# Attention with split scores: two heads at a time on the two halves of the array's rows, and the normalisation moved to VectorE

## The chip, the cores and the metric

The kernel runs on one core of one Trainium2 chip. The metric is device time in microseconds of one execution; where a kernel was run several times the median is given. A core has five engines with a queue of their own each: TensorE (PE, with its weight loads shown apart as PEld), VectorE (DVE), ScalarE (ACT), GpSimd (POOL) and SyncE (SP, which here only starts the loads of weights). Every engine takes its instructions in the order in which they were written into its queue, and waits on semaphores for the others.

## The reference: what is computed

A trunk of two layers on 256 tokens of 1024 features, in float32. Each layer is a SwiGLU half-step, a mixer, and another SwiGLU half-step, every one behind an RMSNorm and added to the residual stream. Both mixers have 16 heads of 64. Cut to what matters here:

```python
def swiglu(h, w_gate, w_up, w_down):              # 1024 -> 2816 -> 1024
    return (silu(h @ w_gate) * (h @ w_up)) @ w_down

# mixer A: three dilated causal windows, merged per head by their softmax denominators
s = einsum('...qd,...kd->...qk', q, k) * HEAD_DIM ** -0.5;  p = softmax(where(mask, s, -inf))
o = einsum('...qk,...kd->...qd', p, v);  out = o @ w_o

# mixer B: q from its own projection, k and v computed once from the stream after layer 0;
# with 256 tokens there is one block, so that it is plain causal attention
```

In the kernel both are one softmax per head over the keys: the three windows of mixer A become one additive mask (the logarithm of how many windows hold the pair), and mixer B has the causal mask.

## The kernel before, in words

Names and lines are those of the profile. 256 tokens are two tiles of 128 (`t`), the 1024 features eight blocks of 128. The precision comes from splitting: `parts_of` (L90) writes a float32 value as the sum of two float32r parts, the high one by a copy on ACT (L92), the low one by a subtraction on DVE (L94, or L96 with a scale). Weights are split in the same way by `pieces_of` (L154 on ACT, L155 on DVE, 1024 columns at a time, eight pieces in flight), and a product of two split operands is three float32r products: high by high, high by low, low by high (L183, L185, L187 for tokens on partitions; L192, L193, L195 for features on partitions).

Only the scores are not split. `attend` takes a list of groups of four heads and, per head:

- `scores` (L490): q^T and k^T are plain float32, two heads to a tile of 128 partitions, so that one head has 64 rows. Two products: queries of tile 0 with 128 keys, queries of tile 1 with 256 keys, both into one PSUM bank. The program's float32 product is two passes of the array, so that the trace has four matmuls for a head.
- softmax: a masked, scaled negative with the row maximum on DVE (L492, two instructions with an accumulator read each), the exponential with the row sum on ACT (L495, two), the reciprocal on DVE (L497), and the normalisation on **ACT** (L499, one instruction of 128 columns and one of 256).
- three transposes of p (L510) into a PSUM bank, split into `pT` by `parts_of`.
- the product with v (L527 to L530): v is split into high and low parts, which are two stationary operands. Each is loaded with **both heads of a pair** side by side (128 columns), of which only the own half of the result is used. Four matmuls of 512, 256, 256 and 256 columns. The two halves of the result's bank are added by a copy on ACT (L536) and an addition on DVE (L537).
- each pair's o^T is split (`oT`) and is an input of the output projection `out_t` (L418 to L420), which holds four of the five PSUM banks of the pool `accp`.

PSUM has eight banks: five in `accp`, three in `trp`. A score bank, a bank of transposes of p and a bank of transposes of q and k all come from `trp`.

What sets the order: `weave` merges two generators of steps. The main one is `attend`, the filling one is the projection of the next group's q, k and v (mixer A, groups 0 to 2), or the output projection (mixer A, group 3), or the second half of the queries' projection followed by the output projection (mixer B, all four groups as one stream). Each step yields the time of TensorE that its author put to it, and the merge spreads the one stream over the other; so TensorE always has other products between a head's scores, its transposes and its product with v. `AHEAD` is how many heads have their scores ahead of their transposes, `LATE` how many heads the product with v comes late. The framework then fixes one order of instructions for each engine when the program is built. In mixer A a group is opened by the projection of q and k: `turned` scales and rotates them (L459, L451 to L454), `transposed` (L468) turns them and copies them on DVE to `qT` and `kT` (L470). Mixer B reads k^T from `kTb`, written by the shared projection, and splits v for each group when it comes to it (`bv`, L92 and L94).

Of the kernel before, what the change touches and what calls it, by code (L numbers as in the profile page):

```python
# [15 lines left out]
P = 128  # L16
S = 256
# [11 lines left out]
AHEAD = 3  # heads whose scores are there ahead of their transposes  # L29
LATE = 1  # heads by which the products with v follow the transposes  # L30
EXTRA = 1  # blocks of an output projection that wait for the end of the attention
# [10 lines left out]
def shape_constants():  # L42
    """Rotary tables and attention masks: functions of the shapes alone."""
# [23 lines left out]
def trunk(ctx: ExitStack, tc: tile.TileContext, a: dict, out: bass.AP):  # L67
# [6 lines left out]
    ap_ = ctx.enter_context(tc.tile_pool(name="ap", bufs=22))  # L74
# [15 lines left out]
    def parts_of(hi, lo, src, scale=1.0):  # L90
        """src * scale as the sum of two float32r parts."""
# [48 lines left out]
    def unit(name, k, n, srcs):  # L140
        """Loads [P, k, n] of weights and splits it into pieces of 1024 columns."""
# [18 lines left out]
    def opening(wg, wu, before):  # L160
        """The first two units, in parts of two blocks of rows that arrive with the parts of x."""
# [18 lines left out]
    def product(accs, xh, xl, ws, first, last):  # L180
        """accs[i] += x @ ws[i] for one block of 128 rows of the contraction."""
# [7 lines left out]
    def product_t(ac, wh, wl, x, first, last):  # L189
        """ac[:, 0] + ac[:, 1] += w^T @ x^T for one block of 128 rows of the contraction; x: [P, hi and lo, S]."""  # L190
# [69 lines left out]
    def some(steps, n):  # L260
        """The next n steps."""
# [5 lines left out]
    def hurried(steps, factor):  # L267
        """Steps that a weave takes sooner than their time says."""
# [3 lines left out]
    def weave(main, main_total, fill, fill_total):  # L272
        """Traces both streams, the steps of the one spread over those of the other."""
# [14 lines left out]
    def down_t(name, w, blocks, norm):  # L288
        """h^T += 0.5 * (blocks @ w)^T, one block of 128 features after another, each followed by its norm."""
# [14 lines left out]
    def joined(ac, name):  # L304
        """The two parts of a transposed product, added."""
# [5 lines left out]
    def ffn_blocks(name, wg, wu, norm, first=None):  # L311
        """(silu(x @ wg) * (x @ wu))^T in blocks of 128 features: [P, hi and lo, S]."""
# [94 lines left out]
    def out_t(name, w, blocks, norm, tail=4 - EXTRA):  # L407
        """h^T += (blocks @ w)^T, two blocks of 128 features to a bank; the last blocks of rows bank by bank."""
# [35 lines left out]
    def rotate(v, t, name):  # L444
        """Partial rotary in place on v: [P tokens, slots, DH]."""
# [314 lines left out]
```

## Time and profile before

| | |
|---|---|
| time, median of 3 runs | 1018.86 us (1018.77 to 1019.18) |
| span of the profiled execution | 1016.9 us |
| what lies around the span (median less span) | 2.0 us |
| instructions in the span | 15214 |
| HBM read | 173.99 MB, 172 GB/s over the span |
| mixer A, from the first score product to the last of the output projection | 215.5 to 322.6 us |
| mixer B, from the first score product to the last of the output projection | 759.1 to 822.0 us |

How to read the profile: the page's first part gives each engine's busy time, but a busy TensorE is not a full one, because matmuls overlap and their ends are modelled. How much time a matmul really takes from the others is read from the start of one to the start of the next. On DVE and ACT too an instruction may start before the last one's end is shown. "Windows" give the busy time of every engine in a stretch. The chain of waits is followed back from the last instruction. In a group's row, the figure behind the bar is the idle time just before its instructions, and what ended it.

### The profile page before, as it was taken

What the parts mean: (1) busy time and instruction counts of PE and PEld (TensorE: products, weight loads), DVE (VectorE), ACT (ScalarE), POOL (GpSimd) and SP (SyncE); (2) the same over time, 40 slices, a digit from 0 to 9 for tenths busy, and PEclk for the clock granted to TensorE, in tenths of its full rate; (3) what the DMA queues carried; (4) which work ended last, traced back from release to release, by engine and by line L of the source; (5) the groups of instructions that cost most, each with busy time, mean ns of one, the idle gap of its engine ahead of it and who ended that gap; (6) DMA issues with size and microseconds to landing.
All of it is one profiled execution on the core that took longest, in us unless ns stands there. A gap on an engine that the chain in (4) does not pass through costs nothing.

```text
span 1016.9 us, 15214 instructions
## 1 busy us (share of the span) xinstructions
PE 1005.8 (99%) x5739; PEld 862.0 (85%) x5739; DVE 713.5 (70%) x1284; ACT 613.4 (60%) x1128; POOL 150.1 (15%) x147
## 2 busy tenths in 40 slices
PE   8999999999999999999999999999999999999997
PEld 6888888888889888888888888888877888888886
DVE  7977765667767787766576777766577878777542
ACT  7756554567776565555455566655459966665531
POOL 3221201000002212210000121210100032212000
PEclk9999999999999999999999999999999999999999
DMA  9875545743333656545475565654561255555511
GB/s 309 259 256 166 191 167 182 231 146 124 124 124 126 203 171 205 194 159 186 167 241 171 177 195 166 196 189 150 211 208 46 85 161 187 187 169 205 187 61 42
DMA packets 152154, 176.03 MB, mean 173 GB/s; under 512 B 3472, under 2 KB 139920, under 8 KB 152080
## 3 DMA queue, kind: packets, MB, share of 16 engines
q1 hardware_dynamic: 151648, 174.50, 52.6%
q8 instruction: 45, 0.74, 0.3%
q10 hardware_dynamic: 432, 0.55, 0.2%
q14 instruction: 29, 0.24, 0.1%
HBM read 173.99 MB, written 1.05 MB: 172 GB/s over the span
## 4 chain that ended last, share of the span: by engine, by line
PE 96%; ACT 1%; DVE 1%; POOL 1%; issue 0%; DMA 0%; POOLq 0%
PE f_u L193 16%; PE f_g L193 15%; PE dn_f L193 12%; PE f_u L195 7%; PE f_g L195 7%; PE dn_f L195 6%; PE dn_f_d L185 2%; PE dn_f_d L183 2%; PE dn_f_d L187 2%; PE qk L183 2%; PE qk L187 1%; PE kv L183 1%; PE qk L185 1%; PE kv L187 1%; PE kv L185 1%; PE s_a L490 1%
## 5 line engine op out<-in xcount | busy, mean ns | idle before, releaser
L193 PE MATMUL f_u<-x_n,wh_f_u 128*128 128x512 f32 x688 | 252.1, 398 | 0.2 <-DVE j_f_g L308 0.2
L193 PE MATMUL f_g<-x_n,wh_f_g 128*128 128x512 f32 x688 | 251.9, 398 | 0.0
L193 PE MATMUL dn_f<-act_f,wh_f 128*128 128x512 f32 x528 | 184.9, 398 | 0.0
L195 PE MATMUL f_g<-x_n,wl_f_g 128*128 128x256 f32 x602 | 168.9, 281 | 0.0
L195 PE MATMUL f_u<-x_n,wl_f_u 128*128 128x256 f32 x602 | 168.8, 281 | 0.0
L327 POOL TENSOR_TENSOR j_f_u<-j_f_u,r_n 128x256 f32<-128x256 f32 x88 | 102.9, 1170 | 406.5 <-DVE j_f_u L308 345.5
L193 PEld LDWEIGHTS f_u<-x_n,wh_f_u 128*128 128x128 f32 x688 | 129.3, 188 | 24.7 <-DVE j_f_g L308 0.6
L193 PEld LDWEIGHTS f_g<-x_n,wh_f_g 128*128 128x128 f32 x688 | 129.6, 188 | 23.5
L195 PE MATMUL dn_f<-act_f,wl_f 128*128 128x256 f32 x504 | 141.5, 281 | 0.0
L195 PEld LDWEIGHTS f_u<-x_n,wl_f_u 128*128 128x128 f32 x602 | 113.7, 189 | 4.0 <-DVE wl_f_u L155 0.3
L195 PEld LDWEIGHTS f_g<-x_n,wl_f_g 128*128 128x128 f32 x602 | 113.8, 189 | 3.4
L193 PEld LDWEIGHTS dn_f<-act_f,wh_f 128*128 128x128 f32 x528 | 97.8, 188 | 22.1
L155 DVE TENSOR_TENSOR wl_f_g<-raw_f_g,wh_f_g 128x1024 fp32r<-128x1024 f32 x86 | 106.6, 1243 | 7.8 <-ACT wh_f_g L154 5.6
L155 DVE TENSOR_TENSOR wl_f_u<-raw_f_u,wh_f_u 128x1024 fp32r<-128x1024 f32 x86 | 105.2, 1225 | 9.0 <-ACT wh_f_u L154 7.3
L154 ACT ACTIVATE wh_f_g<-raw_f_g 128x1024 fp32r<-128x1024 f32 x86 | 90.1, 1054 | 25.5 <-PE f_g L193 19.7
L195 PEld LDWEIGHTS dn_f<-act_f,wl_f 128*128 128x128 f32 x504 | 95.2, 189 | 1.1
L154 ACT ACTIVATE wh_f_u<-raw_f_u 128x1024 fp32r<-128x1024 f32 x86 | 90.2, 1053 | 8.7 <-PE f_g L193 6.9
L225 POOL TENSOR_TENSOR ss_n<-ss_n,sq_n 128x256 f32<-128x256 f32 x42 | 36.3, 863 | 372.2 <-ACT sq_n L224 186.3
L155 DVE TENSOR_TENSOR wl_f<-raw_f,wh_f 128x1024 fp32r<-128x1024 f32 x72 | 80.9, 1144 | 10.4 <-ACT wh_f L154 8.9
L154 ACT ACTIVATE wh_f<-raw_f 128x1024 fp32r<-128x1024 f32 x72 | 70.0, 985 | 17.3 <-PE dn_f L193 10.9
L328 DVE TENSOR_TENSOR j_f_g<-j_f_g,j_f_u 128x256 f32<-128x256 f32 x88 | 37.6, 429 | 59.0 <-POOL j_f_u L327 57.8
L92 ACT ACTIVATE x_n<-hT,gT 128x256 fp32r<-128x256 f32 x56 | 26.8, 505 | 80.3 <-DVE hT L301 73.3
(207 smaller groups left out, 1841.1 us busy)
## 6 DMA issues: line engine op xcount, KB each, us to landing
raw_f_g<-in_ffn_w_gate_dram SPq DMA_DIRECT2D x43, 1024.0 KB, 5.4
raw_f_u<-in_ffn_w_up_dram SPq DMA_DIRECT2D x43, 1024.0 KB, 5.3
raw_f<-in_ffn_w_down_dram SPq DMA_DIRECT2D x24, 1024.0 KB, 5.1
raw_f_d<-in_ffn_w_down_dram SPq DMA_DIRECT2D x11, 1024.0 KB, 5.0
raw_f<-in_ffn_w_down_dram SPq DMA_DIRECT2D x12, 768.0 KB, 4.4
raw_qk<-in_a_w_qkv_dram SPq DMA_DIRECT2D x16, 512.0 KB, 4.7
raw_kv<-in_kv_w_dram SPq DMA_DIRECT2D x8, 1024.0 KB, 5.2
raw_v<-in_a_w_qkv_dram SPq DMA_DIRECT2D x4, 1024.0 KB, 5.2
```

The source lines that it names most:

```text
L92: nc.scalar.activation(hi, src, AF.Copy, scale=scale)
L154: nc.scalar.activation(wh, r, AF.Copy)
L155: nc.vector.tensor_sub(wl, r, wh.bitcast(F32))
L183: nc.tensor.matmul(ac, xh, wh, start=first, stop=False)
L185: nc.tensor.matmul(ac, xh, wl, start=False, stop=False)
L187: nc.tensor.matmul(ac, xl, wh, start=False, stop=last)
L193: nc.tensor.matmul(ac, wh, flat(x), start=first, stop=last)
L195: nc.tensor.matmul(ac[:, :S], wl, x[:, 0, :], start=False, stop=False)
L225: nc.gpsimd.tensor_tensor(self.ss, self.ss, sq, op=ALU.add)
L327: nc.gpsimd.tensor_tensor(u, u, norm.row, op=ALU.mult)
L328: nc.vector.tensor_mul(g, g, u)
L490: nc.tensor.matmul(ps[:, seg], qT[p0:p0 + DH, b, t, :], kh[:, :(t + 1) * P], start=True, stop=True)
```

## The change

- **Scores in three products.** `transposed` writes q^T and k^T as two float32r parts (ACT copy, DVE subtraction) where it was one DVE copy. In mixer B k^T of a group is split from `kTb` when the group is reached (`bk`). `scores` takes a pair of heads: for each tile of queries and each of the three part products one matmul for the head on rows 0 to 63 and one for the head on rows 64 to 127, into two PSUM banks. That is 12 matmuls for a pair, on alternating halves.
- **Parts of v side by side.** The stationary operand of the product with v holds the high and the low part of one head (64 and 64 columns). Two matmuls of 512 and 256 columns in place of four. The result has four quarters to add: a copy on ACT and two additions on DVE for each head, where it was one addition.
- **p normalised on VectorE.** The two instructions of L499 move from ACT to DVE.
- `AHEAD` is 2 pairs in place of 3 heads; the steps' times in the weave are changed to fit; the pool `ap` has 28 buffers in place of 22; `dynamic_dma_scratch_size=1024`.

In the built program, the loads on SP stand in the same order, and outside the two mixers the engines' instructions are the same, but for a few splits of the next half-step's weights that stand a place earlier or later.

```diff
@@ transposed
         for i, dst in enumerate(dsts):
-            nc.vector.tensor_copy(dst[:, :, t, :],
-                                  tr[:, 2 * i * P:(2 * i + 2) * P].rearrange("p (k n) -> p k n", n=P))
+            src = tr[:, 2 * i * P:(2 * i + 2) * P].rearrange("p (k n) -> p k n", n=P)
+            if isinstance(dst, tuple):
+                parts_of(dst[0][:, :, t, :], dst[1][:, :, t, :], src)
+            else:
+                nc.vector.tensor_copy(dst[:, :, t, :], src)
@@ attend: scores, then soften for each of the two heads
+        def scores(g, b):
+            (qh, ql), (kh, kl), _ = operands(g)
+            ps = [trt(f"s_{name}{g}_{2 * b + i}") for i in range(2)]
+            for t, seg in enumerate(segs):
+                for n, (q, k) in enumerate(((qh, kh), (qh, kl), (ql, kh))):
+                    for i in range(2):
+                        own = slice(i * DH, (i + 1) * DH)
+                        nc.tensor.matmul(ps[i][:, seg], q[own, b, t, :],
+                                         k[own, b].rearrange("p t n -> p (t n)")[:, :(t + 1) * P],
+                                         start=n == 0, stop=n == 2)
+            for i in range(2):
+                soften(g, 2 * b + i, ps[i])
...
             for t, seg in enumerate(segs):
-                nc.scalar.activation(sm[:, seg], sm[:, seg], AF.Copy, scale=ls[:, t:t + 1])
+                nc.vector.tensor_scalar_mul(sm[:, seg], sm[:, seg], ls[:, t:t + 1])
...
-            (h0, l0), (h1, l1) = [[v[:, i, pair] for i in range(2)] for v in operands(g)[2]]
-            nc.tensor.matmul(po, h0, pT[:, :, :2 * P], start=True, stop=False)
-            nc.tensor.matmul(po[:, :S], l0, pT[:, 0, :2 * P], start=False, stop=False)
-            nc.tensor.matmul(late, h1, pT[:, :, 2 * P:], start=False, stop=False)
-            nc.tensor.matmul(late, l1, pT[:, :, 2 * P:], start=False, stop=True)
+            both = [v[:, j].rearrange("p i d -> p (i d)") for v in operands(g)[2]]
+            nc.tensor.matmul(po, both[0], pT[:, :, :2 * P], start=True, stop=False)
+            nc.tensor.matmul(late, both[1], pT[:, :, 2 * P:], start=False, stop=True)
...
-            own = slice(j % 2 * DH, (j % 2 + 1) * DH)
-            nc.scalar.activation(s[own], po[own, S:], AF.Copy)
-            nc.vector.tensor_add(s[own], po[own, :S], s[own])
+            s = ss[g, j // 2][j % 2 * DH:(j % 2 + 1) * DH]
+            part = s if j % 2 == 0 else etile(f"op_{name}{g}_{j}")[:DH]
+            nc.scalar.activation(part, po[DH:, :S], AF.Copy)
+            nc.vector.tensor_add(part, po[:DH, S:], part)
+            nc.vector.tensor_add(s, po[:DH, :S], part)
@@ mixer_b, operands
+                    ks[g] = split([P, 2, NT, P], f"bk_{g}")
+                    parts_of(ks[g][0], ks[g][1], kTb[:, 2 * g:2 * g + 2])
```

More of the change, by code (lines that the diff above doesn't have):

```diff
@@ L28 @@
 HALF = ROT // 2
-AHEAD = 3
+AHEAD = 2
 LATE = 1
@@ L513, in attend @@
                 yield 0.35
-            if n + AHEAD < len(heads):
-                while operands(heads[n + AHEAD][0]) is None:
+            if n % 2 and n + 2 * AHEAD - 1 < len(heads):
+                g, j = heads[n + 2 * AHEAD - 1]
+                while operands(g) is None:
                     yield None
-                scores(*heads[n + AHEAD])
-                yield 0.65
+                scores(g, j // 2)
+                yield 0.9
             if n < LATE:
@@ L543, in attend, with split @@
                     table(AF.Silu, x[:, 0, 0:1].bitcast(F32))
-    ATT = HG * 1.55
+    def split(shape, name):
+        return tuple(atile(shape, F32R, name=f"{name}{i}") for i in "hl")
+    ATT = HG * 1.15
     def project(ac, pieces, xs, k0):
@@ L641, in turn_in @@
                 for i in range(2):
-                    qTs.append(atile([P, 2, NT, P], name=f"bqT{c}{i}"))
+                    qTs.append(split([P, 2, NT, P], f"bqT{c}{i}"))
             transposed(turn[t], qTs[2 * c:2 * c + 2], t, f"q{c}{t}")
```

42 lines of the change are left out of this document (18 added, 24 removed).

## The prediction

> **What bounds the kernel now.** I read the page first (busy time and the chain), then windows cut at the mixers' stages, then single instructions of TensorE and DVE in order of time.
>
> ```profile
> span 1016.9 us, 15214 instructions
> ...
> PE 1005.8 (99%) x5739; PEld 862.0 (85%) x5739; DVE 713.5 (70%) x1284; ACT 613.4 (60%) x1128; POOL 150.1 (15%) x147
> ...
> PE 96%; ACT 1%; DVE 1%; POOL 1%; issue 0%; DMA 0%; POOLq 0%
> ```
>
> TensorE bounds the whole: 96% of the chain that ended last is matmuls, and DVE has 30% to spare on average. But the change touches only the two mixers, so the average doesn't decide. The windows below begin at the first score product of mixer A's groups 0, 1, 2 and 3 (the last runs to the end of the output projection), and the fifth goes in mixer B from DVE's first instruction on a score to its last on o^T. Columns: length, then busy time and count for PE, PEld, DVE, ACT, POOL, then granted clock, DMA share, GB/s.
>
> ```profile
> 215.50:241.00 25.50, 25.50 (x149) 20.71 (x148) 18.25 (x51) 18.75 (x45) 0.00 (x0) 1.00 0.39 128
> 241.00:266.60 25.60, 25.60 (x150) 20.73 (x149) 18.36 (x51) 18.85 (x45) 0.00 (x0) 1.00 0.37 120
> 266.60:292.20 25.60, 25.60 (x153) 20.98 (x152) 18.30 (x51) 18.79 (x45) 0.00 (x0) 1.00 0.38 123
> 292.20:322.60 30.40, 30.40 (x232) 28.28 (x232) 19.66 (x49) 22.41 (x55) 2.52 (x4) 1.00 0.35 113
> 760.30:818.80 58.50, 57.37 (x370) 46.86 (x369) 44.59 (x148) 52.42 (x154) 0.00 (x0) 1.00 0.28 87
> ```
>
> In mixer A DVE is busy 72% of a group (18.3 of 25.6 us). In mixer B it is 76%, and ACT 90%. So a cut on TensorE is worth its full size only until DVE is full, and it becomes full first in B.
>
> **TensorE: the scores.** What one head costs is read from the starts around it.
>
> ```profile
> 240.71 0.39 PE L187 MATMUL qk<-wh_qk,x_n 128*128 128x512 f32 x1
> 241.03 0.92 PE L490 MATMUL s_a<-kT,qT 64*128 64x128 f32 x4
> 241.88 0.50 PE L183 MATMUL qk<-wh_qk,x_n 128*128 128x512 f32 x1
> 242.22 0.39 PE L185 MATMUL qk<-wl_qk,x_n 128*128 128x512 f32 x1
> 242.45 0.40 PE L187 MATMUL qk<-wh_qk,x_n 128*128 128x512 f32 x1
> ...
> 248.25 0.49 PE L510 MATMUL pt_a<-ident,sm_a 128*128 128x128 f32 x3
> ```
>
> ```profile
> L510 PE MATMUL pt_a<-ident,sm_a 128*128 128x128 f32 x48 | 7.8, 272 | 0.0
> ```
>
> A projection's product takes 0.23 us (242.22 to 242.45). From 240.71 to 242.22 are 1.51 us for two of them and one head: **1.05 us a head**. Three transposes of 128 columns last 0.49, a single one 0.272 in the mean, so one follows the other after 0.11. Two passes of 128 columns at 0.11 and two of 256 at twice that are 0.66; the other 0.39 is an estimate of what it costs to go to 64 rows and back (the array empties, and a weight load shows).
>
> ```profile
> 758.73 0.40 PE L187 MATMUL bq<-wh_bq,x_n 128*128 128x512 f32 x1
> 759.05 0.93 PE L490 MATMUL s_b<-kTb,bqT 64*128 64x128 f32 x8
> 759.91 0.50 PE L183 MATMUL bq<-wh_bq,x_n 128*128 128x512 f32 x1
> 760.25 0.39 PE L185 MATMUL bq<-wl_bq,x_n 128*128 128x512 f32 x1
> ```
>
> Here two heads stand next to each other, on the two halves of the rows, and all eight matmuls take what four did (1.52 us against 1.51). So the halves do run side by side, loads included. A pair of the new kind has six matmuls on each half: three of 128 columns, which a weight load paces like the transposes (0.11), and three of 256 at 0.115 (below): 0.68, with the switch 1.07. This is not shown for float32r on 64 rows; the bounds are 0.68 and twice that (the halves one after another), and I take 0.68, which the nearest row, this pair, says. In the built program's order filling products cut into the pairs: 12 blocks of scores in A for 8 pairs, 11 in B. A: 12 x 0.39 + 8 x 0.68 = 10.1 us for 16 x 1.05 = 16.8, a saving of 6.7. B: 11 x 0.39 + 8 x 0.68 = 9.7, for 14 x 1.05 + 1.06 + one cut of 0.39 = 16.2, a saving of 6.5.
>
> **TensorE: the product with v.**
>
> ```profile
> 767.17 0.40 PE L527 MATMUL po_b<-pT_b,bv 128*128 128x512 f32 x1
> 767.41 0.28 PE L528 MATMUL po_b<-pT_b,bv 128*128 128x256 f32 x1
> 767.53 0.27 PE L529 MATMUL po_b<-pT_b,bv 128*128 128x256 f32 x1
> 767.64 0.28 PE L530 MATMUL po_b<-pT_b,bv 128*128 128x256 f32 x1
> 767.76 0.40 PE L185 MATMUL bq<-wl_bq,x_n 128*128 128x512 f32 x1
> ```
>
> 0.59 us for four; two of the 256-column ones go: 0.23 less a head, 3.7 a mixer. TensorE thus needs **10.4 us less in A** (2.6 a group) and 10.2 less in B.
>
> **DVE: what is added.** DVE starts an instruction before the last one's shown end, so I count from start to start.
>
> ```profile
> 759.16 1.23 DVE L155 TENSOR_TENSOR wl_bo<-raw_bo,wh_bo 128x1024 fp32r<-128x1024 f32 x1
> 760.30 0.28 DVE L492 CUSTOM_DVE_ANT_0 sm_b<-s_b,masks 128x128 f32<-128x128 f32 x1
> ...
> 803.58 0.42 DVE L94 TENSOR_TENSOR oT_b<-o_b,oT_b 128x256 fp32r<-128x256 f32 x1
> 803.92 0.41 DVE L537 TENSOR_TENSOR o_b<-po_b,o_b 64x256 f32<-64x256 f32 x1
> ```
>
> 256 columns take 0.34 (803.58 to 803.92), 1024 take 1.14 (759.16 to 760.30); the overlap is 0.08. The second addition of a head is 0.34. For the normalisation the nearest rows are the two kinds of tensor-by-column product:
>
> ```profile
> L717 DVE TENSOR_TENSOR out<-vb,gfin 128x512 f32<-128x512 f32 x3 | 2.1, 693 | 0.1
> L241 DVE TENSOR_SCALAR diag_n<-ident,c_n 128x128 f32<-128x128 f32 x8 | 1.9, 284 | 2.8 <-POOL c_n L234 2.8
> L727 DVE TENSOR_SCALAR out<-out,rms 128x512 f32<-128x512 f32 x2 | 1.0, 486 | 2.2 <-POOL rms L725 2.2
> ```
>
> With 512 columns, a column of factors takes 486 ns where two tensors take 693. 128 columns last 284, so 256 lie on the line between 284 and 486 at 351. Less the overlap: 0.20 + 0.27 = 0.47 a head; at the two-tensor price it would be 0.55, which is the upper bound. The Trainium skill ("VectorE: DVE Perf Modes", the perf-mode tier table) has float32 in SBUF at double rate for an operation with one tensor and at single rate for two; L717 and L727 agree, and by its rule too the price is the lower one. I take 0.47. So DVE gets **0.81 us more a head, 13.0 a mixer**, and 3.2 a group of A.
>
> What else moves: q and k in A cost DVE a subtraction in place of a copy, of the same size, at no change; ACT gets the copy. ACT loses L499, two instructions a head:
>
> ```profile
> L499 ACT ACTIVATE sm_b<-sm_b,ls_b 128x256 f32<-128x256 f32 x16 | 8.0, 498 | 0.0
> L499 ACT ACTIVATE sm_b<-sm_b,ls_b 128x128 f32<-128x128 f32 x16 | 6.3, 394 | 0.1
> ```
>
> That is 14.3 us a mixer, more than the new copies, so ACT is nowhere the bound after the change. The loads are the same in the same order on SP's queue; the larger pool and the scratch size I cost at nothing, since no instruction is added and every load is a hardware queue's. If the pool's count delayed a tile, DVE would show it as a wait.
>
> **Mixer A.** A group needs 25.6 - 2.6 = 23.0 us of TensorE and 18.3 + 3.2 = 21.5 of DVE: 94%, so TensorE should still lead. Two waits are new. The scores of the next group need k^T of the second token tile in both parts, and its ACT copy stands in ACT's queue behind a split of weights of about 1 us, its subtraction behind another on DVE; TensorE, whose queue behind that product is the next projection, waits some 0.6 us by the order of these queues. So 2.0 a group, 6.0 for three; the first group opens 0.3 later for the same copy. In group 3 the first `pT` subtraction now stands on DVE behind four normalisations (2.2 us with their reciprocals) and a weight split (1.14), and the product with v behind it; of the 5 us that TensorE has between, I count 1.5 us of waiting: 1.1 saved. A: -6.0 + 0.3 - 1.1 = **-6.8 us**. At worst a further microsecond of waiting goes to each group (-3); at best all 10.4 are had.
>
> **Mixer B.** DVE's 44.6 us become 44.6 + 13.0 (heads) + 1.8 (three `bk` of 512 columns, 0.60 each) + 1.1 (one more weight split stands inside the stretch in the built order) + 0.3 (one more part of q) = **60.8 us, in a stretch that now takes 58.5**. TensorE needs 48 there. So B can't get shorter by what TensorE saves: DVE becomes its bound. What remains are DVE's waits:
>
> ```profile
> DVE ls_b L497 <- ACT sm_b L495: 4.4, 8, 1.2
> DVE o_b L537 <- ACT o_b L536: 2.6, 5, 1.5
> ```
>
> DVE now idles 13.9 us of the 58.5. With a full queue most of these waits are over when it gets to them (two pairs of scores are ahead, and ACT is freer). Bounds: none left gives +2.3, all left +16.2. I take 1.7 left, near the full queue, for the row that it is nearest to is the busiest engine of this stretch: 62.5 us, **+4.0**. Behind B nothing moves: the output projection's end waits for the last o^T as before.
>
> The Trainium skill ("TensorEngine Tiling (Array Packing)", PSUM Bottleneck) warns that tiling speeds up TensorE but not the emptying of PSUM, which may become the limit. The sum above has it so in B and not yet in A.
>
> **Sum.** -6.8 + 4.0 = -2.8 us: a span of 1014.1 for 1016.9, and with the 2.0 around it 1016.1 for the median of 1018.86.
>
> **Rivals.** *DVE's load is hidden.* The idle 13.9 us take it up, and B comes out even (+1), A with nearly all (-10): 1018.9 - 9 = 1009.9. For it: DVE is 72% busy in A, and the weight splits for the next half-step could as well be late. Against: 60.8 is over 58.5. Chance 0.18. *DVE's waits stay* (slower). A normalisation stands on DVE directly behind its reciprocal, which waits for ACT's exponential, and the second addition behind the first, which waits for ACT's copy. If the two waits of the last fence stay whole (7.0), B takes 67.8, +9.3; A's groups, with DVE at 94%, lose half their gain (-3.4): +5.9, 1024.8. It decides from a B of 65.3 us on, where A's gain is eaten. For it: DVE waits for exactly these now, and in B the output projection leaves one bank for the product with v, which now comes free only after two additions. Against: these waits are ones of a queue that runs empty. Chance 0.22. *The halves don't run side by side* in float32r, or 128 columns take longer than 0.11: up to 0.68 more a pair, 5.4 in A, while B hides it behind DVE: -2.8 + 5.4, 1021.5. The change then doesn't do what its name says. Against: the eight matmuls at 759.05. Chance 0.13.
>
> **How the numbers follow.** The forecast has 0.47, and its own range is 1012.5 to 1020.5 (A between -9 and -4, B between +2.3 and +7). About 0.2%, 2.0 us, is what a measurement can tell from no change. Of the forecast 0.27 lies below 1016.8, 0.16 within 2.0 us and 0.04 above; with the first rival faster is 0.45. The third gives 0.06 to same and 0.07 to slower, and the second 0.02 and 0.20: same 0.24, slower 0.31. The range 1008.5 to 1025 leaves out the far ends of the two outer rivals.
>
> **What would show it.** In the profile after: score rows of about 1 us for 12 matmuls (over 1.5 would be the third rival); A's groups 23 to 24 us from first score to first score; B from DVE's first score instruction to its last o^T 61 to 65 us, DVE over 93% busy there and TensorE with gaps, ACT below 80%; normalisations of 128 and 256 columns at about 284 and 351 ns. It is wrong if B is shorter than 58 us, or if a group of A still takes 25 us.

## The result, and the profile after

The changed kernel takes **1026.53 us** (median of 4 runs, 1025.34 to 1030.37) against 1018.87 for the kernel before: a ratio of 1.0080, 95% interval 1.0068 to 1.0092. It is 0.8% slower, where the prediction had 1016.1 and a range up to 1025.0. Its four executions had mean granted clocks of 0.994, 0.990, 0.987 and 0.994, and their times go with them; the profiled execution is the fastest.

The page of the changed kernel, its first part and its chain:

```profile
span 1023.5 us, 15315 instructions
...
PE 995.4 (97%) x5739; PEld 855.4 (84%) x5739; DVE 741.1 (72%) x1384; ACT 603.3 (59%) x1092; POOL 149.2 (15%) x147
...
PEclk9999999999999999999999999999998999999999
...
PE 91%; DVE 5%; ACT 2%; issue 1%; DMA 0%; POOL 0%; POOLq 0%; ACTq 0%
```

TensorE is busy for 10.4 us less, and yet the span is 6.6 us longer: 5% of the chain is now DVE's, and one slice of the granted clock is below 9. The same windows as before the change: mixer A's four groups, then mixer B from DVE's first instruction on a score to its last on o^T.

```profile
215.89:239.72 23.83, 23.22 (x149) 19.40 (x148) 21.20 (x62) 17.28 (x41) 0.00 (x0) 1.00 0.31 95
239.72:263.71 23.99, 23.38 (x149) 19.37 (x149) 21.43 (x63) 17.30 (x41) 0.00 (x0) 1.00 0.36 132
263.71:287.72 24.01, 23.40 (x152) 19.66 (x151) 21.43 (x63) 17.30 (x41) 0.00 (x0) 1.00 0.40 135
287.72:317.69 29.97, 28.46 (x232) 27.04 (x232) 22.95 (x62) 19.03 (x44) 1.48 (x2) 1.00 0.42 136
754.90:826.30 71.40, 57.22 (x377) 46.60 (x377) 60.74 (x202) 49.01 (x131) 0.00 (x0) 0.93 0.24 79
```

Mixer A ends at 317.69 for 322.60: 4.9 us won. Mixer B, from its first score (754.08) to the end of its output projection (829.04), takes 75.0 us for 63.0: **12.0 lost**. Between and behind them 0.4 is won; together +6.6, the difference of the spans. Over the whole of B's 71.4 us neither TensorE (57.2) nor DVE (60.7) is full, and the granted clock is 0.93. But the mean hides two parts (columns as above):

```profile
760.00:770.00 10.00, 9.59 (x60) 6.87 (x60) 9.62 (x39) 8.41 (x27) 0.00 (x0) 1.00 0.33 106
770.00:780.00 10.00, 7.79 (x50) 6.26 (x51) 9.84 (x40) 8.54 (x22) 0.00 (x0) 1.00 0.00 0
780.00:790.00 10.00, 7.25 (x56) 6.09 (x55) 9.94 (x36) 6.71 (x19) 0.00 (x0) 0.83 0.53 174
```

For these 30 us DVE is busy 98% of the time (29.4 us); behind them, to 826.30, it is busy for 27.0 of 36.3 us. The product with v of the seventh head starts 34.5 us after B's first score, where before the change it was 29.9: 4.6 of the 12.0 us are lost by then, with DVE full, and 7.4 after it. What TensorE waits for in B, first in the changed kernel, then in the kernel before (columns: total, times, longest):

```profile
PE po_b L540 <- DVE o_b L549: 7.9, 5, 3.3
PE ot_bo L418 <- ACT oT_b L92: 1.9, 2, 1.3
PE ot_bo L419 <- DVE oT_b L94: 1.9, 4, 0.6
```

```profile
PE ot_bo L419 <- DVE oT_b L94: 0.6, 1, 0.6
PE po_b L527 <- DVE o_b L537: 0.2, 1, 0.2
PE ot_bo L418 <- ACT oT_b L92: 0.2, 1, 0.2
```

All three are ends of one chain: the product with v, its copy on ACT, the additions on DVE, and then either the PSUM bank (L540) or o^T for the output projection (L418, L419). (Of the four quarters in the product's bank three are added; the low part of p times the low part of v isn't read. So a head has one copy and two additions.) Single instructions show how that chain got longer. First one head before the change, then one after it (the columns of a timeline: start, length, engine, instruction):

```profile
808.72 0.38 ACT L536 ACTIVATE o_b<-po_b 64x256 f32<-64x256 f32 x1 [0.20 <-PE po_b L530]
809.13 0.42 DVE L537 TENSOR_TENSOR o_b<-po_b,o_b 64x256 f32<-64x256 f32 x1 [0.15 <-ACT o_b L536]
809.51 0.56 DVE L94 TENSOR_TENSOR pT_b<-pt_b,pT_b 128x384 fp32r<-128x384 f32 x1
...
809.68 0.42 PE L527 MATMUL po_b<-pT_b,bv 128*128 128x512 f32 x1
```

```profile
817.16 0.38 ACT L547 ACTIVATE op_b<-po_b 64x256 f32<-64x256 f32 x1 [2.45 <-PE po_b L541]
817.58 0.42 DVE L548 TENSOR_TENSOR op_b<-po_b,op_b 64x256 f32<-64x256 f32 x1 [1.44 <-ACT op_b L547]
...
818.10 0.56 DVE L94 TENSOR_TENSOR pT_b<-pt_b,pT_b 128x384 fp32r<-128x384 f32 x1
818.69 0.42 DVE L549 TENSOR_TENSOR o_b<-po_b,op_b 64x256 f32<-64x256 f32 x1
...
819.25 0.47 PE L540 MATMUL po_b<-pT_b,bv 128*128 128x512 f32 x1 [1.16 <-DVE o_b L549]
```

Before, the next product started 0.96 us after the copy's start, beside the split of the next head's p. Now it starts 2.09 us after it: at this head the built order puts that split (0.56) **between** the two additions, so that the second addition costs the chain not its own 0.4 but a whole microsecond. It isn't the same at every head: the additions at 820.61 and 821.05 follow each other directly, and between those at 779.99 and 782.32 stand splits of q, k and v. From the start of a product with v to the end of its last addition a head of B takes 3.89 us in the mean of 16, for 2.60 before.

Then the clock. These windows of the changed kernel cut B at the places where it changes (last three columns: granted clock, DMA share, GB/s); below them stand the last matmul ahead of the first drop and the next one:

```profile
783.20:786.60 3.40, 2.58 (x20) 1.75 (x18) 3.40 (x13) 2.94 (x11) 0.00 (x0) 1.00 0.11 33
786.60:793.40 6.80, 4.87 (x22) 4.80 (x23) 5.62 (x26) 3.32 (x12) 0.00 (x0) 0.50 0.45 154
793.40:800.30 6.90, 3.63 (x27) 2.89 (x26) 4.15 (x9) 3.82 (x8) 0.00 (x0) 0.99 0.00 0
800.30:803.70 3.40, 3.40 (x21) 3.08 (x20) 3.05 (x14) 1.54 (x7) 0.00 (x0) 0.50 0.01 2
```

```profile
786.16 0.27 PE L493 MATMUL s_b<-bk_2h,bqT10l 64*128 64x256 f32 x1
788.53 0.77 PE L540 MATMUL po_b<-pT_b,bv 128*128 128x512 f32 x1 [2.09 <-DVE o_b L549]
```

TensorE's clock is halved for 6.8 and for 3.4 us, and a product of 256 columns of the output projection then takes 0.21 us from start to start where it took 0.12. The first drop (786.62) comes 0.2 us into the gap of 2.1 us, so that this gap can't be its cause; ahead of it are gaps of 0.4 to 0.7 us, the last at 783.81. The second (800.28) follows a gap of 3.3 us. The gap of 2.1 us is a wait for a second addition that started at 787.97, on a DVE that had not paused since the copy at 785.99: the end of a weight split and the normalisations of two heads stood ahead of its two additions or between them.

### The profile page after: what moved, and what is told of

It reads as the page before. It is cut to its first block, busy times and chain, and to the rows that moved or that the text cites. A ratio compares the mean times of both kernels' runs of the same rounds, so it can differ in the third digit from the quotient of the medians.

```text
span 1023.5 us, 15315 instructions
## 1 busy us (share of the span) xinstructions
PE 995.4 (97%) x5739; PEld 855.4 (84%) x5739; DVE 741.1 (72%) x1384; ACT 603.3 (59%) x1092; POOL 149.2 (15%) x147
## 4 chain that ended last, share of the span: by engine, by line
PE 91%; DVE 5%; ACT 2%; issue 1%; DMA 0%; POOL 0%; POOLq 0%; ACTq 0%
PE f_u L193 16%; PE f_g L193 16%; PE dn_f L193 12%; PE f_u L195 7%; PE f_g L195 7%; PE dn_f L195 6%; PE dn_f_d L183 2%; PE dn_f_d L185 2%; PE dn_f_d L187 2%; PE qk L183 2%; PE kv L183 1%; PE kv L187 1%; PE kv L185 1%; PE qk L187 1%; PE qk L185 1%; PE f_u L192 1%
## 5 line engine op out<-in xcount | busy, mean ns | idle before, releaser
L155 DVE TENSOR_TENSOR wl_f<-raw_f,wh_f 128x1024 fp32r<-128x1024 f32 x72 | 80.9, 1145 | 10.4 <-ACT wh_f L154 8.9
```

What stands on the lines that cost most here:

```text
L155: nc.vector.tensor_sub(wl, r, wh.bitcast(F32))
```

## The experiments

Mixers A and B below are from the first score to the end of the output projection in each run's profile; "clock" is B's mean granted clock. Ratios are against the kernel before on the same chip, with 95% intervals.

**Each part alone and each pair of parts.** With before and after these are all eight combinations.

| scores in pairs | v side by side | p normalised on | run | us | ratio | A | B | clock |
|---|---|---|---|---|---|---|---|---|
| no | no | ACT | before | 1018.9 | | 107.1 | 63.0 | 1.00 |
| no | no | DVE | n_only | 1018.9 | 1.0000 (0.9991 to 1.0008) | 107.3 | 62.9 | 1.00 |
| no | yes | ACT | v_only | 1023.8 | 1.0044 (1.0029 to 1.0059) | 103.5 | 72.5 | 0.95 |
| no | yes | DVE | vn_only | 1022.7 | 1.0037 (1.0023 to 1.0050) | 103.5 | 70.6 | 0.95 |
| yes | no | ACT | scores_only | 1025.1 | 1.0059 (1.0047 to 1.0072) | 108.9 | 67.8 | 0.95 |
| yes | no | DVE | pv_back | 1020.6 | 1.0020 (1.0012 to 1.0029) | 108.0 | 64.2 | 1.00 |
| yes | yes | ACT | norm_back | 1031.1 | 1.0119 (1.0106 to 1.0133) | 101.9 | 81.6 | 0.88 |
| yes | yes | DVE | after | 1026.5 | 1.0080 (1.0068 to 1.0092) | 101.8 | 75.0 | 0.93 |

The edits are parts of the diff, taken alone or undone; norm_back, for one, is the changed kernel with

```diff
-                nc.vector.tensor_scalar_mul(sm[:, seg], sm[:, seg], ls[:, t:t + 1])
+                nc.scalar.activation(sm[:, seg], sm[:, seg], AF.Copy, scale=ls[:, t:t + 1])
```

> The changed kernel with one part undone: the normalisation of p is on ACT again; scores and product with v stay changed. DVE loses 16 x 0.62 us of busy time (7.5 us by starts) in each mixer. Load theory (mixer B lasts as long as DVE's work plus a near-constant rest): B comes back by about 7.5 of its 12 us, A by about 0.5, so about 1018.5. Bank theory (B is set by the ring through the one PSUM bank of the product with v: product, ACT copy, two additions on DVE, next product): the ring keeps its two additions, DVE only gets to them sooner; B comes back by 2 to 4, so about 1023. Clock theory (the gaps matter because TensorE's clock falls to half after them): granted clock back at 1.00 in B only if the gaps go, then some 4 us on top of either.

> The changed kernel with the product with v undone: four products and one addition a head, parts of v laid out as before; scores in pairs and the normalisation on DVE stay. DVE loses 5.4 us a mixer, TensorE gets 3.7 more a mixer. Load theory: B comes back by 5.4, A loses up to 3: about 1024. Bank theory: the ring is one addition shorter (0.34 to 0.42 us a head and whatever stands between the two), so B comes back by 7 to 10, A loses up to 3: about 1019 to 1021.

> Only the scores in pairs: the normalisation on ACT and the product with v as in the kernel before. TensorE needs 6.7 us less in A and 6.5 less in B, DVE gets only the splits of k and q in B (3.2 us): 48 of 58.5. Both theories: A shorter by 5 to 6, B by 0 to 5, in all 1008 to 1014; the halves' rate is then worth what the prediction put on it. If it isn't below 1016, something in the pairs themselves (two PSUM banks at once, heads ahead in twos) costs time in B.

> The kernel before with the two other parts: the parts of v side by side (two products, two additions) and the normalisation on DVE; scores as before, three heads ahead. DVE gets 13.0 us a mixer (57.6 in B's 58.5), TensorE 3.7 less. Load theory: B +2 to +5, A -2 to -3: 1018 to 1021. Bank theory: B +8 to +12, A -2 to -3: 1024 to 1028.

> The kernel before with only the parts of v side by side (two products, one more addition a head); scores and normalisation as before. TensorE 3.7 us less a mixer, DVE 5.4 more (50 of B's 58.5). Load theory: DVE isn't full, B +0 to +1, A -3.7: 1015 to 1016.5. Bank theory (the second addition holds the one bank of the product with v in B): B +6 to +10, A -3.7: 1021 to 1025.

> The kernel before with only the normalisation on DVE. DVE 7.5 us more a mixer (52 of B's 58.5), ACT 14 less, TensorE as before. Load theory (as the prediction had it): B +0 to +2, A 0: 1019 to 1021. Other theory, drawn from the runs of the parts (with scores in pairs the kernel was 4.5 us faster with the normalisation on DVE than on ACT): the chain score, maximum, exponential, normalisation, transposes is shorter on DVE, B -1 to -4: 1015 to 1018.

The load theory, on which the prediction rests, falls as an account of B's 12 us. Giving the normalisation back to ACT should have returned 7 us of B; it cost 6.6 (the bank theory, with 2 to 4 us back, missed this as well). v_only and pv_back came out where the bank theory had them, vn_only (1022.7) between the two forecasts, n_only at the lower end of the load theory's, and scores_only, for which both had 1008 to 1014, took 1025.1. The two parts that load DVE, alone, in mixer B (first n_only, then v_only; third busy time is DVE's, then ACT's):

```profile
759.28:822.17 62.89, 62.41 (x405) 51.13 (x405) 53.53 (x188) 45.64 (x129) 0.00 (x0) 1.00 0.24 78
```

```profile
755.80:828.31 72.51, 63.31 (x373) 50.05 (x373) 54.28 (x171) 57.74 (x161) 0.00 (x0) 0.95 0.25 82
```

DVE's work is the same to 0.8 us, and one leaves B where it was while the other adds 9.5. So it is the product with v, and not what DVE has to do. In A the same edit saves 3.6 us, where 3.7 was forecast. The normalisation on DVE, forecast as the dearest part of DVE's load, costs nothing alone, and with one or both of the other parts it saves 2.0 to 6.6 us of B. Scores in pairs alone add 4.8 to B with ACT normalising and 1.3 with DVE doing it:

```profile
760.86:828.66 67.80, 62.53 (x437) 53.60 (x437) 50.16 (x161) 59.26 (x170) 0.00 (x0) 0.95 0.23 73
```

```profile
759.92:824.13 64.21, 59.27 (x437) 50.37 (x437) 58.58 (x196) 51.65 (x145) 2.29 (x3) 1.00 0.25 78
```

(scores_only, then pv_back): DVE has 8.4 us more in the second, ACT 7.6 less, and B is shorter by 3.6. So ACT's queue had a part in it, into which the change puts the copies of the parts of k and q.

Is it then the full DVE of B's first part? The next table has the 30 us that begin 5 us after B's first score (one_add, half_norm_dve and add_in_chain come below).

| run | additions a head in the chain | DVE busy in 30 us | B |
|---|---|---|---|
| before | 1 | 24.2 | 63.0 |
| pv_back | 1 | 29.3 | 64.2 |
| half_norm_dve | 1 | 29.4 | 63.8 |
| one_add | 1 | 28.3 | 66.8 |
| v_only | 2 | 24.1 | 72.5 |
| add_in_chain | 2 | 25.4 | 75.1 |
| after | 2 | 29.4 | 75.0 |

A DVE as full as in the changed kernel, with one addition, goes with a B of 63.8 and 64.2; a DVE with some 5 us to spare, with two, with 72.5 and 75.1.

In A, too, the parts don't simply add up. Scores in pairs alone made A longer, by 1.8 us (scores_only) and 0.9 (pv_back), where 5 to 6 less was expected; only with v side by side they shorten it, by 1.7 (vn_only to after). So most of A's 5.3 us is the product with v. In both runs TensorE waits 2.4 us for k^T, and 2.7 us (scores_only) and 2.0 us (pv_back) for a split of p, where the changed kernel has one such wait, of 0.9 us. The row of scores_only:

```profile
PE po_a L541 <- DVE pT_a L94: 2.7, 4, 0.7
```

**The order, the bank, and the number of additions.** v_only took over the step times of the merge with the change; v_old_weave puts them back.

```diff
-            yield 0.35
+            yield 0.55
...
-    ATT = HG * 1.35
+    ATT = HG * 1.55
```

> The kernel with only the parts of v side by side, with the step times of the weave put back to those of the kernel before, so that the two streams are merged in the old order. If the merge's order had a part in B's +9.5: 1018 to 1021 (1023.8 without this edit). Bank theory: no difference beyond 1.5 us.

1028.0 us (1.0085, 1.0071 to 1.0099), A 103.9, B 74.4. The old merge doesn't help; it isn't the order of the two streams.

early_free gives the bank back one addition sooner:

```diff
             nc.scalar.activation(part, po[DH:, :S], AF.Copy)
+            nc.scalar.activation(top, po[:DH, :S], AF.Copy)
             nc.vector.tensor_add(part, po[:DH, S:], part)
-            nc.vector.tensor_add(s, po[:DH, :S], part)
+            nc.vector.tensor_add(s, top, part)
...
```

> The changed kernel with the bank of the product with v given back before the second addition: ACT copies the first quarter too (one more copy of 64 x 256 a head, about 0.38 us), and the second addition reads that copy from SBUF. DVE has the same two additions and the same load, ACT 6 us more a mixer. Bank theory (how long the one bank is held decides B): B 3 to 7 us shorter, about 1020 to 1024, and TensorE's waits for the second addition are gone. Load theory, or the additions themselves: no gain, 1026 to 1028.

1026.7 us (1.0073, 1.0060 to 1.0086), B 75.0: no gain. TensorE's waits in its B:

```profile
PE ot_bo L418 <- ACT oT_b L92: 5.5, 6, 1.4
PE po_b L540 <- DVE op_b L550: 2.1, 4, 0.8
```

The wait for the bank went from 7.9 to 2.1, and the wait for o^T from 1.9 to 5.5. So the bank theory falls in the form in which I had it: with the bank free, TensorE stands at the other end of the same chain. (The edit isn't clean: ACT's extra copies are 3.4 us in B and make A 1.8 us longer, 103.6, B's mean clock is 0.91, and each head takes one or two more tiles from a pool of five.)

one_add takes the second addition out, by sending the low part of p only through the high part of v; half_norm_dve does the same with two heads to a bank.

```diff
-            nc.tensor.matmul(po, both[0], pT[:, :, :2 * P], start=True, stop=False)
-            nc.tensor.matmul(late, both[1], pT[:, :, 2 * P:], start=False, stop=True)
+            nc.tensor.matmul(po, both[0], pT[:, 0, :2 * P], start=True, stop=False)
+            nc.tensor.matmul(po[:DH], vs[0][:, j, 0], pT[:, 1, :2 * P], start=False, stop=False)
+            nc.tensor.matmul(po[:DH, P:], vs[1][:, j, 0], pT[:, 1, 2 * P:], start=False, stop=False)
+            nc.tensor.matmul(po[:, P:], both[1], pT[:, 0, 2 * P:], start=False, stop=True)
...
-            nc.vector.tensor_add(part, po[:DH, S:], part)
-            nc.vector.tensor_add(s, po[:DH, :S], part)
+            nc.vector.tensor_add(s, po[:DH], part)
```

> The changed kernel with another product with v: the parts of v stay side by side for the high part of p, and the low part of p goes only through the high part of v (64 columns of the array), on to the same half of the bank: four products of 256, 256, 128 and 128 columns, one copy on ACT and one addition on DVE a head; low by low is left out, as in the kernel before the fourth quarter was. TensorE some 0.1 us more a head than the changed kernel, DVE 5.4 us less a mixer. Each head has its own bank, as before. Load theory: B -5, A +1.5: 1023. Bank theory: the ring is back at one addition: B -9 to -11, A +1.5: 1017 to 1019.

> As the kernel with one addition, but two heads share a PSUM bank, a half of 256 columns each, so that every second product with v doesn't wait for a bank. Work on every engine the same as in that kernel. Bank theory: B another 2 to 5 us shorter than with a bank for each head. If it is the additions alone (or the load), no difference within 1 us.

one_add: 1020.3 us (1.0012, 1.0003 to 1.0020), A 104.8, B 66.8 at a clock of 0.95. half_norm_dve: 1018.2 (0.9994, 0.9986 to 1.0003), A 105.5, B 63.8 at 1.00. One addition less gives back 8.2 us of B; in A it loses 3.0, where 1.5 was expected. The other 3.0 for the half banks can't be told from the clock: the half clock of one_add, 6.8 us, is worth up to 3.4, and half_norm_dve has none.

**In the chain or beside it.** Both are the kernel before with one more DVE instruction of 64 x 256 for each head of mixer B; nothing else in the source differs. First add_beside, then add_in_chain:

```diff
             nc.vector.tensor_add(s[own], po[own, :S], s[own])
+            if name == "b":
+                nc.vector.tensor_add(etile(f"ox_{name}{g}_{j}")[own], masks[own, 0, :S], masks[own, 1, :S])
```

```diff
-            nc.vector.tensor_add(s[own], po[own, :S], s[own])
+            if name == "b":
+                more = etile(f"ox_{name}{g}_{j}")
+                nc.vector.tensor_add(more[own], po[own, :S], s[own])
+                nc.vector.tensor_add(s[own], po[own, :S], more[own])
+            else:
+                nc.vector.tensor_add(s[own], po[own, :S], s[own])
```

> The kernel before, with a second addition of the same size for each head in mixer B, beside the chain: it adds two constant tiles into a scratch tile that nobody reads. The number of DVE's instructions and columns is that of the kernel with the addition in the chain. Chain theory: B +0 to +2, 1019 to 1021. Load theory: the same time as with the addition in the chain.

> The kernel before, with a second addition for each head in mixer B alone, in the chain: the first addition goes to a tile of its own, the second adds the first half of the bank again and writes o^T (which changes the result of B). On DVE it stands, as in the changed kernel, behind the split of the next head's p. TensorE's work is that of the kernel before. Chain theory (B is a loop over product with v, copy, addition, o^T or bank, next product; the loop gets longer by the addition and by what stands ahead of it on DVE): B +5 to +10, 1024 to 1029, with half clock in places. Load theory: +0 to +2, 1019 to 1021.

add_beside: 1019.2 us (1.0004, 0.9996 to 1.0013). add_in_chain: **1032.0** (1.0127, 1.0113 to 1.0141). Mixer B of the one and of the other:

```profile
759.07:822.65 63.58, 62.58 (x404) 50.80 (x403) 53.83 (x171) 56.06 (x160) 0.00 (x0) 1.00 0.28 85
```

```profile
759.02:834.15 75.13, 66.41 (x405) 53.81 (x405) 56.26 (x174) 58.03 (x164) 0.38 (x1) 0.96 0.25 80
```

Sixteen instructions of the same size, 6.6 us of DVE: 0.6 us of B beside the chain, 12.1 in it. What TensorE waits for in the second:

```profile
PE s_b L490 <- DVE pT_b L94: 3.4, 2, 2.6
PE ot_bo L419 <- DVE oT_b L94: 1.8, 4, 0.6
PE ot_bo L418 <- ACT oT_b L92: 1.7, 2, 1.3
PE po_b L527 <- DVE o_b L540: 1.5, 2, 1.2
```

5.0 us are the ends of the chain, as above. The other 3.4 are waits for a bank for scores, which a split of p sets free: a longer chain also holds up what stands behind it on DVE. One rival is left in this pair. The framework orders the instructions anew for each program, and from the seventh product with v on TensorE's order differs in all three kernels (up to the sixth it is the same, and that one starts 0.7 us later than before in add_beside, 1.7 in add_in_chain). What an order alone was worth is shown only by v_only and v_old_weave, 1.9 us of B; the pair differs by 11.5.

The mean from product to last addition, measured in the same way in each trace, mostly goes with B's length: 2.46 us (add_beside, B 63.6), 2.60 (before, 63.0), 2.75 (half_norm_dve, 63.8), 2.85 (pv_back, 64.2), 3.01 (one_add, 66.8), 3.44 (v_only, 72.5), 3.47 (add_in_chain, 75.1), 3.89 (after, 75.0). Two runs with more work on ACT fall out of the row: early_free with 4.75 (75.0) and norm_back with 3.93 (81.6).

**The clock.** warm and warm2 are the changed kernel with useless transposes of the unit matrix ahead of products with v in B; warm has six for every head but the last, warm2 has 18, 12, 6 and 8 for the four products with the longest gaps ahead of them.

```diff
+            if name == "b":
+                for _ in range({6: 18, 8: 12, 12: 6, 14: 8}.get(n - LATE, 0)):
+                    nc.tensor.transpose(bank[:, 3 * P:], ident, ident)
```

> The changed kernel with useless work for TensorE in mixer B: six transposes of the unit matrix, into the unused 128 columns of the bank of the transposes of p, before each product with v (15 x 6 x 0.11 = 9.9 us). Clock theory (the gaps let the granted clock fall to a half, and that is a good part of B's 12 us): the gaps are filled, the clock stays at 1.00 and the time falls by 2 to 5 us in spite of the work. If the clock is only a small part: the same time or up to 5 us more.

> The changed kernel with useless transposes of the unit matrix ahead of four products with v in mixer B, at the places of its longest gaps (18 ahead of head 6, 12 ahead of head 8, 6 and 8 ahead of heads 12 and 14; 4.8 us in all, most of it in gaps of 2.1, 3.3, 0.7 and 1.2 us). Clock theory: no drop of the clock at the first gap, and the time falls by 3 to 6 us, to 1021 to 1024. If the clock drops elsewhere instead, or the gaps only move: within 2 us of 1026.5.

warm: 1025.5 us (1.0063, 1.0051 to 1.0075), B 76.2, clock still 0.93: it filled gaps, but a gap of 1.3 us (785.40 to 786.72) stayed, with a drop of the clock behind it at 787.67. So it says little, except that 9.9 us more of TensorE lengthened B by 1.2. warm2: 1023.8 (1.0050, 1.0036 to 1.0063); its B, and where its first 18 transposes ran:

```profile
754.02:827.53 73.51, 63.77 (x449) 53.33 (x449) 62.75 (x208) 51.28 (x138) 0.00 (x0) 0.98 0.26 82
```

```profile
789.07 3.39 PE L542 MATMUL pt_b<-ident 128*128 128x128 f32 x18
```

The built order put these 18 behind the product that they were meant to precede, so that the first gap of 2.1 us (to 788.48) stayed as it was; a drop of 3.4 us came at 789.74, in the middle of the row of transposes. The later drop is gone. With 4.8 us of useless work added, the clock of B rose from 0.93 to 0.98 and the kernel got 2.7 us faster in the median (B by 1.5 in the profiles). So the half clock costs 2.7 us or more. The four executions of the changed kernel point the same way: from a mean clock of 0.994 to one of 0.987 they take 5.0 us longer.

**Pairs or splits.** scores_single has the scores in three products of split operands, but one head at a time, in one bank, three heads ahead; the rest as in scores_only.

```diff
-                    for i in range(2):
-                        own = slice(i * DH, (i + 1) * DH)
-                        nc.tensor.matmul(ps[i][:, seg], q[own, b, t, :],
+                    nc.tensor.matmul(ps[:, seg], q[own, b, t, :],
...
```

> Scores in three float32r products as in the kernel with scores in pairs alone, but one head at a time, in one bank, three heads ahead, in the old merge of the streams; normalisation on ACT and product with v as before. A head's scores are 0.66 us of columns and 0.39 of switching, as before, so TensorE's work is that of the kernel before; the splits of q and k are the new ones. If pairing made B 4.8 us longer: B within 1 us of before, A longer by the waits for k^T, up to 2.4: 1019 to 1022. If the splits did: B +3 to +5, 1023 to 1027.

1027.1 us (1.0080, 1.0068 to 1.0093), A 110.0, B 68.9. So it isn't the pairing (two banks at once) that lengthens B: with split operands one head at a time it is 68.9, in pairs 67.8. Which part of the splits does it, their copies on ACT or their later k^T and q^T, isn't shown.

**The change where it pays.** a_changed has mixer A of the changed kernel and mixer B of the kernel before. best2 has in B also the product of half_norm_dve. best3 is a_changed with the second tile's transposes of q and k one block of products earlier:

```diff
-                    if k == (0, 3)[t]:
+                    if k == (0, 2)[t]:
```

> The change in mixer A alone; mixer B as in the kernel before. The stages of the profiles added: A -5.3, B 0: 1013.5. If A's gain depended on B in some way, or was lost after it, it would be 1017 or more.

> Mixer A as in the changed kernel; mixer B as in the kernel before, except for the product with v with one addition and two heads to a PSUM bank (four products of 256, 256, 128 and 128 columns, 2.1 us less of TensorE in B). If the loops of B leave no room, B stays within 1 us: 1012.5 to 1014.5. If TensorE's work still counts in B, 1011 to 1012.

> The change in mixer A alone (1013.4), with the transposes of q and k of the second token tile one block of the projection of v earlier (0.36 us), so that k^T is there sooner for the next group's scores. The wait of 0.6 us at each of four groups falls by 0.36 if nothing else holds it: 1012.0. If the rotation isn't ready by then, TensorE waits there instead: 1013.4 or more.

a_changed: 1013.4 us (0.9947, 0.9935 to 0.9959), A 101.8, B 63.0, as the stages added. best2: 1014.6 (0.9962, 0.9949 to 0.9974), B 64.3: 2.1 us less of TensorE brings nothing there. best3: **1010.4** (0.9916, 0.9903 to 0.9930), faster than both kernels:

```profile
215.31:313.93 98.62, 96.69 (x679) 85.47 (x679) 87.14 (x247) 70.15 (x163) 1.50 (x2) 1.00 0.40 129
750.41:813.43 63.02, 61.88 (x405) 51.01 (x405) 48.13 (x156) 55.38 (x161) 0.00 (x0) 1.00 0.31 96
```

A is 3.2 us shorter than in a_changed, where 1.4 was expected. The waits for k^T fell from 2.4 to 0.9 us, as expected; three waits like this one are left:

```profile
PE s_a L494 <- DVE kT_2l L95: 0.3, 1, 0.3
```

The rest is the order that this edit brings about: no pair of A is cut by other products any more (8 blocks of 12 matmuls, where there were 12 blocks), and that is four switches of the array's rows less, 1.6 us at the 0.39 of the prediction. From start to start the scores of A, with the switch ahead and behind and with the waits, sum to 2.9 us less.

## Why the prediction was wrong

**What bounds the kernel: right for A, half right for B.** "B can't get shorter by what TensorE saves" was right. "DVE becomes its bound" was right from 760 to 790 us (29.4 of 30) and not behind that: over the whole stretch its share is 85%, where the prediction expected over 93%. And a DVE as full as that, with one addition a head, cost B only 0.8 and 1.2 us (half_norm_dve, pv_back).

**The scores: right for a pair in one run, a little low for a cut one.** A pair in one run, from the last product ahead of it:

```profile
244.49 0.39 PE L187 MATMUL qk<-wh_qk,x_n 128*128 128x512 f32 x1
244.81 0.33 PE L493 MATMUL s_a<-kT_1h,qT_1h 64*128 64x128 f32 x2
...
245.48 0.28 PE L493 MATMUL s_a<-kT_1h,qT_1l 64*128 64x256 f32 x2
245.69 0.50 PE L183 MATMUL qk<-wh_qk,x_n 128*128 128x512 f32 x1
246.03 0.39 PE L185 MATMUL qk<-wl_qk,x_n 128*128 128x512 f32 x1
```

1.54 us from 244.49 to 246.03, less two products of 0.23: 1.08, forecast 1.07. The halves run side by side in float32r (each row stands for two matmuls at one start), and the third rival is out. A pair that other products cut takes 1.70 without its wait for k^T (2.13 and 1.10 from start to start, less 0.61 of waiting and two products of 0.23 each time), where the sum had 1.46: 0.24 more, once in each group of A.

**DVE's prices and load: right.** The normalisation's two instructions:

```profile
L511 DVE TENSOR_SCALAR sm_b<-sm_b,ls_b 128x256 f32<-128x256 f32 x16 | 5.5, 344 | 0.0
L511 DVE TENSOR_SCALAR sm_b<-sm_b,ls_b 128x128 f32<-128x128 f32 x16 | 4.4, 278 | 0.1
```

344 and 278 ns for 351 and 284, and 60.74 us of DVE in B for 60.8.

**Mixer A: right in kind, 1.9 us short.** Forecast -6.8, measured -4.9. The groups gained 1.7, 1.6 and 1.6 for 2.0 each, with the waits for k^T of 0.6 that were forecast:

```profile
217.05 0.39 PE L493 MATMUL s_a<-kT_0h,qT_0h 64*128 64x256 f32 x2 [0.61 <-ACT kT_0h L92]
```

Group 3 gained 0.4 for 1.1, and the entry cost 0.4 for 0.3. Of the 0.3 to 0.4 that each group fell short, 0.24 is its cut pair. The gain holds only for the three parts together: as said above, the scores without the product with v made A longer.

**Mixer B: the step that failed** is the last term of its sum, "I take 1.7 left, near the full queue, for the row that it is nearest to is the busiest engine of this stretch". DVE idled 10.7 us of 71.4, 9.3 of them behind the first part, so that the stretch grew by 12.9 and not by 4.0. (The busiest engine's row, TensorE's 57.4 of 58.5, leaves 1.1; no row gives 1.7.) The reason given, that a full queue finds its waits over, treats DVE's idle time as slack to be used up. The pair of add_beside and add_in_chain shows that it is slack only for work beside the chain. That pair has a DVE that isn't full; that the same holds with a full one is read from half_norm_dve, pv_back and the changed kernel in the table. Work in the chain was priced at its own length (0.34 a head), where its price is the delay of everything behind it: the addition, the split that the built order puts ahead of it, TensorE's wait, and then the half clock. The prediction had the place of the second addition and the single bank in its text, and added them up as load.

**The rivals.** "DVE's waits stay" came nearest, with 1024.8 and the words about the bank that "comes free only after two additions". But what it priced, DVE's waits of 7.0 us, isn't what happened; TensorE's waits are. As the 12 us stand, the runs bound the parts and don't add them: the second addition is worth 8.2 (one_add) to 11.5 (the pair), half clock included, the half clock 2.7 or more, the split scores with the normalisation on DVE 1.3. What holds B at 64 us in half_norm_dve and best2, where TensorE has less to do, stays open; in the 30 us of the table DVE is busy for 29.4 in the first and ACT for 28.9 in the second, but no run tested whether that is it.

The Trainium skill's warning that tiling may make PSUM's emptying the limit ("TensorEngine Tiling (Array Packing)", PSUM Bottleneck) was read as one on throughput. Here it is the latency of emptying that counts: in v_only and add_in_chain, which lost 9.5 and 12.1 us of B, DVE's throughput had room.

## What to carry to other kernels

Before an instruction is put on an engine with idle time, ask whether it lies in a loop that runs round the engines; beside the loop sixteen of them cost 0.6 us here, in the loop the price is its length and that of whatever the queue has ahead of it, once per turn. A cheaper product that needs one more step behind it pays where TensorE has independent work (here in mixer A: 3.6 us of 3.7) and costs where its next work hangs on that step (mixer B: 9.5 us lost). A mean over a stage can hide a part in which an engine is full; cut the stage before saying that none is. And split a change by stage before it is judged: the same diff took 1026.5 us in both mixers and 1013.4 in mixer A alone, for 1018.9 without it.

## What the runs showed of the hardware

The granted clock was halved in spans of 3.4 us or twice or three times that, and only where TensorE had gaps in the 3.4 us ahead. Within a trace its changes lie whole multiples of 3.41 us apart (786.62, 793.45, 800.28 and 803.69 in the changed kernel; in norm_back all eight changes from 770.87 to 835.72). The Trainium skill ("TensorE: Matmul & The Clock Gate", What's actually happening) has a free-running window of 3413 ns, and the lengths agree. The Trainium skill's advice ("TensorE: Matmul & The Clock Gate", Why this matters for your kernels), no gaps over some 3 us between bursts of matmuls, is too lax for this case. A drop followed a gap of 1.3 us in warm and one of 0.8 in scores_single, and the first drop of the changed kernel came with a gap of 0.7 and 0.2 us of the next in the 3.4 us ahead. Not every gap of that length was followed by one (1.33 us at 823.76 in the changed kernel, 1.4 in half_norm_dve and 1.2 in pv_back were not), so that what it takes isn't shown; nor is whether transposes count as work for it, since the drop in warm2 came within a row of them. Here times scatter with the drops: the changed kernel's four runs lie 5 us apart, those of the kernel before 0.4.
